# A down-projection computed as seven products of halved matrices instead of eight column-and-token blocks

## The chip, the core and the metric

The kernel runs on one core of a Trainium2 chip. A core has five engines with an instruction queue each, and each queue is worked off strictly in order: PE (TensorE, matrix products), DVE (VectorE), ACT (ScalarE), POOL (GpSimd), and SP (SyncE), which here only issues DMA transfers. Engines wait for each other through semaphores. SBUF is the on-chip memory of 128 partitions; PSUM is the accumulator memory of eight banks of 128x512 fp32 values, which PE writes. The metric is the device time of one execution in microseconds (us); less is better. TensorE's clock can be throttled; the profile gives the granted clock as a share of full speed.

## The reference

One layer of a diffusion backbone over 2048 latent tokens of width 1024 and 256 context tokens, batch 1, everything in fp32. A mixer (a 2-D Fourier branch and a bidirectional gated recurrence, merged by gates and projected) is followed by a convolutional feed-forward network of width 2816 on the 32x64 latent grid, and the result is normalised:

```python
def conv_ffn(h, w_up, conv_w, conv_b, w_down, rows, cols):
    z = (h @ w_up).reshape(b, rows, cols, 2 * D_FF)
    z = depthwise_3x3_conv(z, conv_w) + conv_b
    return (silu(z[..., :D_FF]) * z[..., D_FF:]) @ w_down

x = x + gate_2 * conv_ffn(modulate(rmsnorm(x, norm2_g), shift_2, scale_2), ...)
out = rmsnorm(x, final_g)
```

Here `gate_2` is a vector over the 1024 output columns (the sixth modulation vector, "m5" in the kernel), and `D_FF` is 2816 = 22 x 128. The change concerns the last product, 2048 x 2816 times 2816 x 1024, the gate behind it, the residual sum and the final norm.

## The kernel before, in words

fp32 matrices are multiplied with three matmuls of a faster format for each product: every operand is split into a high part (a cast by ACT) and a low part (raw minus high, by POOL or DVE), and PE adds high x high, high x low and low x high in PSUM (`split`, L100 to L103, `mm3`, L142 to L149). One matmul is a 128x128 stationary tile against 512 moving columns.

Earlier phases (projections, Fourier branch, recurrence, merge, output projection) are not touched. They leave the residual stream in 16 tiles `dX` in DRAM and the normalised input of the feed-forward network, split, in SBUF tiles of a pool with eight large slots H0 to H7.

**Up-projection** (`phase3`): for each of 22 pairs of 128-column blocks, two "halves" (gate column block and value column block), 44 in all. A half is 96 matmuls that fill four banks (`za` and `zb` alternate), over weights loaded by SP (two loads of 256 KB, `rw`), cast by ACT and subtracted by POOL (`load_w`). Two weight tiles exist, so the weights of half n+2 are split while half n+1 is computed. When a half's matmuls end, ACT computes the centre tap with the bias (`ac`, L1029) and one other tap (`be`, L1032) of the 3x3 convolution; DVE adds seven more taps from PSUM to `ac` (L1061), and only when they are done may the half after next write those four banks again; POOL adds `be` (L1037). Behind the second half ACT applies SiLU to the first, POOL multiplies the two (L1046, `gate`) and SP stores the result `dZ[j]`, 128x2048, to DRAM.

**Down-projection** (`down`): eight groups, two column halves by four groups of 512 tokens. A group runs over 22 blocks k of the feed-forward width with four banks, 12 matmuls a k: 2112 in all. `load_g` loads 128x512 of `dZ[k]`, ACT casts, POOL subtracts; `load_wd` does the same for the weights, and in the second column half multiplies them by `m5` beforehand. `evict` adds a finished bank to the residual that it loads from `dX`; the first column half goes back to DRAM (`dX2`) multiplied by the final norm's gain, and in the second column half each token tile is normalised and stored to the output.

The order in which instructions stand in each engine's queue is set by a scheduler from the program's order, from priorities and from when it expects operands and buffers to be ready; `issue_after` holds instructions back behind a named one. A buffer of a pool with `bufs=n` is reused in turn and waits for its last reader.

Of the kernel before, what the change touches and what calls it, by code (L numbers as in the profile page):

```python
# [94 lines left out]
class Layer:  # L95
# [56 lines left out]
    def run(self):  # L152
        tc, nc = self.tc, self.nc
        with ExitStack() as es:
# [14 lines left out]
            pr = tc.tile_pool(name="pr", bufs=1, reuse_waits="tile", side="right")  # L169
            self.pr = pr.__enter__()  # L170
# [3 lines left out]
            self.down(last, (p5, pw, pr))  # L174
            hpool.__exit__(None, None, None)

    def scratch(self):
# [15 lines left out]
        self.dX2 = [t([P, TB], f"dX2{i}") for i in range(16)]  # L193
# [806 lines left out]
    def phase3(self, p5):  # L1000


        tc, nc, a = self.tc, self.nc, self.a
        for j in range(NF):
            acc = []
            for half in range(2):
# [12 lines left out]
                end = jj == 2 * NF - 1  # L1019
                if end:  # L1020

                    self.wd, self.first = [], []
                    self.load_raw()
                    for k in range(6):
                        self.load_wd(0, k)
                        if k < 3:
                            self.first.append(self.load_g(0, k))
# [36 lines left out]
    def load_wd(self, gi, k, times=None):  # L1064

        c = gi // NB
        cs = slice(c * TB, (c + 1) * TB)
        src = self.a["ffn_down"]
        if k % 4 == 0:
            self.wt = self.ph.tile([P, 4, 2, TB], F32R, name=f"wd{c}{k}", tag=f"H{(6 * c + k // 4) % 8}")  # L1070
        w = self.wt[:, k % 4]
        if gi == 0:
            self.split(w[:, 0, :], w[:, 1, :], self.wraw[k], None if k < 8 else self.nc.vector)
        else:
            self.load_split(w[:, 0, :], w[:, 1, :], src[0, k * P:(k + 1) * P, cs], self.nc.vector, self.p6, 2, times, "wr")
        self.wd.append(w)

    def load_raw(self):


        self.wraw = []
        src = self.a["ffn_down"]
        for pool, tag, n in ((self.pw, "w", 4), (self.ph, "H6", 8), (self.ph, "H7", 8), (self.pw, "w", 2)):
            t = pool.tile([P, 8 if n == 8 else 4, TB], F32, name="wraw", tag=tag, bufs=1 if n == 8 else 2)
            for i in range(0, n, 2):
                k = len(self.wraw)
                self.nc.sync.dma_start(t[:, i:i + 2, :], src[0, k * P:(k + 2) * P, :TB].rearrange("(k p) c -> p k c", p=P))
                self.wraw += [t[:, i, :], t[:, i + 1, :]]

    def load_g(self, gi, k):  # L1090


        tg = gi % NB
        early = gi == 0 or gi == 1 and k < 3
        pool, nb = (self.pr, 3) if early else (self.p6, 5)
        gh = pool.tile([P, TB], F32R, name="gh", tag="gh", bufs=nb)
        gl = pool.tile([P, TB], F32R, name="gl", tag="gl", bufs=nb)
        if early and (gi or k >= 3):
            q = k if gi else (k - 3) % 4
            if q == 0:  # L1100
                self.graw = self.p5.tile([P, 4, TB], F32, name="graw", tag="be", bufs=2)
                for i in range(3 if gi else min(4, NF - k)):
                    self.last_load = self.nc.sync.dma_start(self.graw[:, i, :], self.dZ[k + i][:, tg * TB:(tg + 1) * TB])
            self.split(gh, gl, self.graw[:, q, :])
        else:
            self.load_split(gh, gl, self.dZ[k][:, tg * TB:(tg + 1) * TB], None, pool, 2 if early else 4)
        return gh, gl

    def down(self, last, pools):


        tc, nc, a = self.tc, self.nc, self.a
        wd = self.wd
        with ExitStack() as es:
            ps = []

            def evict(gi, accs):
# [111 lines left out]
```

## Time and profile before

| | us |
|---|---|
| median of three runs (lowest, highest) | 3133.27 (3123.41, 3134.48) |
| the profiled execution's own time | 3133.75 |
| its span, first to last instruction | 3131.9 |
| start of the up-projection's second half (first half's matmuls end) | 1688.4 |
| first matmul of the down-projection | 2623.8 |
| PE busy / DVE busy / POOL busy / ACT busy in the span | 3075.3 / 1750.7 / 963.4 / 935.8 |

The granted clock is 0.994 on average over the profiled execution. In the profile, a group of instructions is told by its line, engine, operation and tiles (out<-in), with count, busy time, mean length, and the idle time of that engine ahead of it with what ended it. PEld is the loading of stationary tiles, which runs beside the matmuls.

### The profile page before, as it was taken

What the parts mean: (1) busy time and instruction counts of PE and PEld (TensorE: products, weight loads), DVE (VectorE), ACT (ScalarE), POOL (GpSimd) and SP (SyncE); (2) the same over time, 40 slices, a digit from 0 to 9 for tenths busy, and PEclk for the clock granted to TensorE, in tenths of its full rate; (3) what the DMA queues carried; (4) which work ended last, traced back from release to release, by engine and by line L of the source; (5) the groups of instructions that cost most, each with busy time, mean ns of one, the idle gap of its engine ahead of it and who ended that gap; (6) DMA issues with size and microseconds to landing.
All of it is one profiled execution on the core that took longest, in us unless ns stands there. A gap on an engine that the chain in (4) does not pass through costs nothing.

```text
span 3131.9 us, 38972 instructions
## 1 busy us (share of the span) xinstructions
PE 3075.3 (98%) x14955; PEld 2561.1 (82%) x14955; DVE 1750.7 (56%) x2475; ACT 935.8 (30%) x1513; POOL 963.4 (31%) x568
## 2 busy tenths in 40 slices
PE   8999999999999999999999999999999999999998
PEld 5987788888888888877877888888888887788887
DVE  6365533566666640366665777777777777224113
ACT  4322111233333321234433222222222223223222
POOL 2200010000000001343443444344443446455443
PEclk9999999999999999999999999999999999999999
DMA  6255544423223322556561111111111114546443
GB/s 250 87 172 185 187 153 154 140 99 111 95 92 108 105 85 96 198 186 210 180 190 61 55 58 34 54 54 48 54 34 54 54 47 155 168 135 205 149 149 133
DMA packets 284043, 374.69 MB, mean 120 GB/s; under 512 B 20731, under 2 KB 158802, under 8 KB 279506
## 3 DMA queue, kind: packets, MB, share of 16 engines
q1 hardware_dynamic: 283666, 372.15, 36.0%
q8 instruction: 118, 1.93, 0.3%
q14 instruction: 67, 0.55, 0.1%
q0 software_dynamic: 192, 0.06, 0.0%
HBM read 270.68 MB, written 101.45 MB: 119 GB/s over the span
## 4 chain that ended last, share of the span: by engine, by line
PE 91%; DVE 4%; DMA 2%; issue 1%; ACT 1%; POOL 1%; SPq 0%; DVEq 0%; ACTq 0%; POOLq 0%
PE z L148 10%; PE z L147 10%; PE z L146 10%; PE pj L146 10%; PE pj L148 10%; PE pj L147 10%; PE dn L1198 5%; PE dn L1196 5%; PE dn L1197 5%; PE pa L788 4%; PE wo L946 2%; PE wo L947 2%; PE wo L945 2%; PE kv L660 1%; PE pj L379 1%
## 5 line engine op out<-in xcount | busy, mean ns | idle before, releaser
L1061 DVE SCALAR_TENSOR_TENSOR ac<-z,cw,ac 128x1953 f32<-128x1953 f32 (+2 forms) x309 | 703.0, 2275 | 257.0 <-ACT be L1032 242.4
L147 PE MATMUL z<-h,w_up 128*128 128x512 f32 x1408 | 548.8, 390 | 0.0
L146 PE MATMUL z<-h,w_up 128*128 128x512 f32 x1408 | 548.7, 390 | 0.0
L148 PE MATMUL z<-h,w_up 128*128 128x512 f32 x1408 | 548.7, 390 | 0.0
L1037 POOL TENSOR_TENSOR ac<-ac,be 128x1984 f32<-128x1984 f32 x43 | 192.4, 4474 | 434.5 <-DVE ac L1061 421.3
L147 PEld LDWEIGHTS z<-h,w_up 128*128 128x128 f32 x1408 | 264.4, 188 | 54.7
L148 PEld LDWEIGHTS z<-h,w_up 128*128 128x128 f32 x1408 | 264.4, 188 | 54.7
L146 PEld LDWEIGHTS z<-h,w_up 128*128 128x128 f32 x1408 | 264.4, 188 | 54.4
L1198 PE MATMUL dn<-wd,gl 128*128 128x512 f32 x704 | 279.2, 397 | 4.3 <-POOL gl L103 4.3
L1029 ACT ACTIVATE ac<-z,vt,cw 128x2048 f32<-128x2048 f32 x44 | 90.9, 2065 | 636.9 <-PE z L148 636.9
L1196 PE MATMUL dn<-wd,gh 128*128 128x512 f32 x704 | 279.0, 396 | 1.0 <-ACT gh L102 1.0
L103 POOL TENSOR_TENSOR gl<-rw,gh 128x512 fp32r<-128x512 f32 x154 | 207.2, 1353 | 233.6 <-ACT gh L102 213.6
L1197 PE MATMUL dn<-wd,gh 128*128 128x512 f32 x704 | 278.6, 396 | 0.0
L494 ACT ACTIVATE ev<-pj 128x512 f32<-128x512 f32 (+1 forms) x136 | 79.6, 585 | 369.0 <-PE pj L148 334.1
L102 ACT CAST gh<-rw 128x512 fp32r<-128x512 f32 x154 | 94.4, 618 | 245.6 <-PE dn L1197 179.1
L1198 PEld LDWEIGHTS dn<-wd,gl 128*128 128x128 f32 x704 | 133.3, 189 | 36.0 <-POOL gl L103 5.6
L1196 PEld LDWEIGHTS dn<-wd,gh 128*128 128x128 f32 x704 | 133.5, 190 | 31.9 <-ACT gh L102 1.4
L1197 PEld LDWEIGHTS dn<-wd,gh 128*128 128x128 f32 x704 | 133.6, 190 | 30.6
L103 POOL TENSOR_TENSOR w_up<-rw,w_up 128x512 fp32r<-128x512 f32 x88 | 112.8, 1306 | 90.6 <-ACT w_up L102 90.6
L788 PEld LDWEIGHTS pa<-bQ,bkc 128*128 128x128 f32 x896 | 120.6, 191 | 17.0 <-issue 10.6
L788 PE MATMUL pa<-bQ,bkc 128*128 128x128 f32 x896 | 127.5, 286 | 1.2
L103 POOL TENSOR_TENSOR wab<-rw,wab 128x512 fp32r<-128x512 f32 x64 | 93.5, 1480 | 110.4 <-ACT wab L102 110.4
(324 smaller groups left out, 6192.9 us busy)
## 6 DMA issues: line engine op xcount, KB each, us to landing
rw<-dZ SPq DMA_DIRECT2D x154, 256.0 KB, 3.2
rw<-in_ffn_up_dram SPq DMA_DIRECT2D x88, 256.0 KB, 3.6
dZ<-ac SPq DMA_DIRECT2D x22, 1024.0 KB, 4.4
rw<-in_w_in_dram SPq DMA_DIRECT2D x72, 256.0 KB, 3.2
maw<-in_ada_w_dram SPq DMA_DIRECT2D x64, 256.0 KB, 3.2
rw<-in_w_out_dram SPq DMA_DIRECT2D x64, 256.0 KB, 2.7
x<-dX SPq DMA_DIRECT2D x48, 256.0 KB, 5.4
x<-in_x_dram SPq DMA_DIRECT2D x20, 512.0 KB, 6.6
```

Of the source, the lines that this page charges most:

```text
L102: self.nc.scalar.copy(hi, raw)
L103: (eng or self.nc.gpsimd).tensor_tensor(lo, raw, hi, op=SUB)
L146: self.nc.tensor.matmul(ps, lh, rh, start=start and i == 0, stop=False)
L147: self.nc.tensor.matmul(ps, lh, rl, start=False, stop=False)
L148: mm = self.nc.tensor.matmul(ps, ll, rh, start=False, stop=stop and i == last)
L788: mm = nc.tensor.matmul(pa[:, c], kc[:, c], fap(Q, w * P, [(2 * m, nw), (W + m, 2), (1, m)]), start=True, stop=True)
L1029: self.centre = nc.scalar.activation(ac, z, AF.Identity, scale=self.cw[:, 4, jj:jj + 1], bias=self.v("cb", jj))
L1037: nc.gpsimd.tensor_tensor(ac[:, :SEQ - 64], ac[:, :SEQ - 64], be[:, 64:], op=ADD)
L1061: nc.vector.scalar_tensor_tensor(o, z3[:, r0 + dy:r1 + dy, c0 + dx:c1 + dx], self.cw[:, k, jj:jj + 1], o, op0=MUL, op1=ADD)
L1196: nc.tensor.matmul(accs[i], gh[:, t], wh, start=(kk == 0), stop=False)
L1197: nc.tensor.matmul(accs[i], gh[:, t], wl, start=False, stop=False)
L1198: nc.tensor.matmul(accs[i], gl[:, t], wh, start=False, stop=(kk == NF - 1))
```

## The change

The product of the gated activations G (2048 x 2816) and the weights W (2816 x 1024) is cut into halves of the tokens, of the feed-forward width and of the columns. Instead of eight products of quarter matrices, seven are formed, each from sums or differences of at most two quarters of G and of at most two quarters of W, and each is added to or subtracted from up to two quarters of the result (`PRODUCTS`). One product covers 1024 tokens in all eight banks, 11 steps k of 24 matmuls: 7 x 11 x 24 = 1848 matmuls.

- A step's operands (`operand`): one or two loads of 512 KB of `dZ`, a DVE sum or difference of 128x1024 where there are two, a cast and a POOL subtraction of 128x1024; one or two loads of 256 KB of weights, a DVE sum or difference of 128x512 where there are two, a cast and a POOL subtraction of 128x512. They are asked for five steps ahead. Of the seven products, the third and sixth have two quarters of G and one of W, the fifth one and two, the second, fourth and seventh two and two. The first has one quarter of G, and its weights are prepared beforehand.
- The gate m5 is multiplied into all of `ffn_down` beforehand (`gated_weights`, 22 pieces: SP loads 512 KB, POOL multiplies 128x1024 by m5, SP stores 512 KB to `dV5`), and the first product's weights are prepared beforehand too (`first_weights`, 11 pieces: two loads of 256 KB, a POOL subtraction, a split, and a store to `dW` issued by POOL). Both stand inside the up-projection: the program names them at its halves 5 to 26 and 29 to 39. The pieces share two buffers `ws`, and the split one buffer `wsr`.
- The residual lies in four quarter tiles in SBUF, in slots of the H pool; a finished bank is added to them (`evict`, one or two DVE instructions of 128x512 a bank). The reload through `dX2` and the DVE multiplication by m5 in the down-projection are gone. The second half of the tokens is normalised during the sixth product (`half_done`), the rest bank by bank at the end.
- In the last two steps of a product (five in the last product) the matmuls go bank by bank.

```diff
                 end = jj == 2 * NF - 1
+                jt = 2 * j + half
+                if 4 <= jt < 4 + NF:
+                    self.gated_weights(p5, jt - 4)
+                elif 28 <= jt < 28 + KH:
+                    self.first_weights(p5, jt - 28)
                 if end:
-                    self.load_raw()
...
+                    self.first_operands(p5, range(3))
                 self.centre = nc.scalar.activation(ac, z, AF.Identity, ...)
...
-    def load_wd(self, gi, k, times=None):
-    def load_raw(self):
-    def load_g(self, gi, k):
...
+    def gated_weights(self, p5, k):
+        raw = p5.tile([P, D], F32, name="ws", tag="ws", bufs=2)
+        nc.sync.dma_start(raw, self.a["ffn_down"][0, k * P:(k + 1) * P, :])
+        nc.gpsimd.tensor_tensor(raw, raw, self.m5, op=MUL)
+        nc.sync.dma_start(self.dV5[k], raw)
+
+    def first_weights(self, p5, k):
+        raw = p5.tile([P, 2, TB], F32, name="ws", tag="ws", bufs=2)
+        self.load_terms(raw, self.weight_terms(PRODUCTS[0], k))
+        nc.gpsimd.tensor_tensor(raw[:, 1, :], raw[:, 1, :], raw[:, 0, :], op=SUB)
+        w = p5.tile([P, 2, TB], F32R, name="wsr", tag="wsr", bufs=1)
+        self.split(w[:, 0, :], w[:, 1, :], raw[:, 1, :])
+        nc.gpsimd.dma_start(self.dW[k], w)
+
+    def operand(self, idx):
+        p, k = divmod(idx, KH)
+        prod = PRODUCTS[p]
...
+        w = self.p6.tile([P, 2, TB], F32R, name="w", tag="w", bufs=6)
+        rg = self.p6.tile([P, 2, 2 * TB], F32, name="rg", tag="rg", bufs=3)
+        self.load_terms(rg, [self.dZ[KH * kh + k][:, 2 * th * TB:2 * (th + 1) * TB] for th, kh, _ in prod[0]])
+        if p == 0:
+            nc.gpsimd.dma_start(w, self.dW[k])
+        else:
+            rw = self.p6.tile([P, 2, TB], F32, name="rv", tag="rv", bufs=3)
+            self.load_terms(rw, self.weight_terms(prod, k))
+        if len(prod[0]) == 2:
+            nc.vector.tensor_tensor(rg[:, 1, :], rg[:, 1, :], rg[:, 0, :], op=prod[0][1][2])
+        self.split(g[:, 0, :], g[:, 1, :], rg[:, 1, :])
+        if p:
+            if len(prod[1]) == 2:
+                nc.vector.tensor_tensor(rw[:, 1, :], rw[:, 1, :], rw[:, 0, :], op=prod[1][1][2])
+            self.split(w[:, 0, :], w[:, 1, :], rw[:, 1, :])
+
+    def product(self, idx, acc, i):
+        nc.tensor.matmul(acc, gh[:, t], wh, start=(k == 0), stop=False)
+        nc.tensor.matmul(acc, gh[:, t], wl, start=False, stop=False)
+        nc.tensor.matmul(acc, gl[:, t], wh, start=False, stop=(k == KH - 1))
...
+            def evict(p, i):
+                for th, c, op in PRODUCTS[p][2]:
+                    x = X[th, c][:, i, :]
+                    nc.vector.tensor_tensor(x, x, accs[i], op=op)
+                if p < 6:
+                    return
+                square(0, 0, i)
...
+            for p in range(7):
...
+                late = 2 if p < 6 else 5
+                for k in range(8 if p == 0 else 0, KH):
+                    idx = KH * p + k
+                    if idx + AHEAD < 7 * KH:
+                        self.operand(idx + AHEAD)
+                    if k < KH - late:
+                        for i in range(8):
+                            self.product(idx, accs[i], i)
...
+                for i in range(8):
+                    for k in range(KH - late, KH):
+                        self.product(KH * p + k, accs[i], i)
+                    evict(p, i)
+
+PRODUCTS = [([(0, 0, ADD)], [(0, 1, ADD), (1, 1, SUB)], [(0, 1, ADD), (1, 1, ADD)]),
...
+KH, AHEAD = NF // 2, 5
```

The scheduler does not leave the new pieces at the halves at which the program names them. All 22 gated pieces and all 11 of the first product's weights stand within the first eleven halves of the up-projection, in the queues of SP, POOL and ACT. First, POOL's queue. Before, from the addition of `be` of the third half on (`gl` is the low part of a first operand of the down-projection):

```order
L1037 TENSOR_TENSOR ac<-ac,be 128x1984
L103 TENSOR_TENSOR w_up_14818<-rw,w_up_14818 128x512 x2
L1037 TENSOR_TENSOR ac<-ac,be 128x1984
L1046 TENSOR_TENSOR ac<-ac 128x2048
L103 TENSOR_TENSOR w_up_14939<-rw,w_up_14939 128x512 x2
L103 TENSOR_TENSOR gl<-rw,gh 128x512
```

The same stretch with the change. The line numbers have shifted by two (L1039 is the addition of `be`, L1048 the gate product); L1071 is the product with m5, L1079 the subtraction in `first_weights`, L1082 its store:

```order
L1039 TENSOR_TENSOR ac<-ac,be 128x1984
L1071 TENSOR_TENSOR ws<-ws,m_14232 128x1024
L103 TENSOR_TENSOR w_up_14838<-rw,w_up_14838 128x512 x2
L1071 TENSOR_TENSOR ws<-ws,m_14232 128x1024 x4
L1039 TENSOR_TENSOR ac<-ac,be 128x1984
L1048 TENSOR_TENSOR ac<-ac 128x2048
L1071 TENSOR_TENSOR ws<-ws,m_14232 128x1024 x2
L103 TENSOR_TENSOR w_up_14963<-rw,w_up_14963 128x512 x2
L1079 TENSOR_TENSOR ws<-ws 128x512
L103 TENSOR_TENSOR wsr<-ws,wsr 128x512
```

So the low parts of the weights for the next halves (w_up_14838 for the sixth half, w_up_14963 for the seventh) now stand behind products with m5, each of which needs a landed load and a buffer that a store has freed.

Second, ACT's queue with the change, from the split of the seventh half's weights on (before, it holds only the casts `w_up`, `ac`, `be` and the SiLU there):

```order
L102 CAST w_up_14963<-rw 128x512 x2
L102 CAST wsr<-ws 128x512 x2
L1031 ACTIVATE ac<-z,vt,cw 128x2048
L1034 ACTIVATE be<-z,cw 128x2048
L1036 ACTIVATE ac<-ac 128x2048
L102 CAST w_up_15085<-rw 128x512 x2
L102 CAST wsr<-ws 128x512 x4
L1031 ACTIVATE ac<-z,vt,cw 128x2048
L1034 ACTIVATE be<-z,cw 128x2048
```

The casts into `wsr`, which has one buffer that only the store to `dW` frees, stand ahead of the centre tap (L1031) of the sixth half, and four more ahead of that of the seventh.

Third, DVE's queue at the end of the first product (L1132 and L1136 are the sums of the next product's operands, L1212 the additions of finished banks to the quarter tiles):

```order
L1136 TENSOR_TENSOR rv<-rv 128x512
L1132 TENSOR_TENSOR rg<-rg 128x1024 x2
L1136 TENSOR_TENSOR rv<-rv 128x512
L1132 TENSOR_TENSOR rg<-rg 128x1024
L1212 TENSOR_TENSOR x_19865<-x_19865,dn 128x512
L1136 TENSOR_TENSOR rv<-rv 128x512
L1212 TENSOR_TENSOR x_19874<-x_19874,dn 128x512
```

Additions to the result now stand between operand sums that wait for loads; before, no DVE instruction of the down-projection's operands had two loaded terms.

More of the change, by code (lines that the diff above doesn't have):

```diff
@@ L173, in run @@
             last = self.phase3(self.p5)
-            self.down(last, (p5, pw, pr))
+            self.down(last, (p5, pw))
             hpool.__exit__(None, None, None)
@@ L192, in scratch @@
         self.dS0 = [t([P, P], f"dS0{h}") for h in range(4)]
-        self.dX2 = [t([P, TB], f"dX2{i}") for i in range(16)]
+        self.dW = [dr.tile([P, 2, TB], F32R, name=f"dW{k}") for k in range(KH)]
+        self.dV5 = [t([P, D], f"dV5{k}") for k in range(NF)]
         self.dU = t([P, 16, TB], "dU")
@@ L1003, in phase3 @@
         tc, nc, a = self.tc, self.nc, self.a
+        self.m5 = p5.tile([P, D], F32, name="m5")
+        nc.sync.dma_start(self.m5, self.dm5)
         for j in range(NF):
@@ L1078, in load_raw @@
-    def load_raw(self):
[L1081 to L1088, printed above, removed]
@@ L1090, in load_g @@
-    def load_g(self, gi, k):
[L1093 to L1107, printed above, removed]
+    def gated_weights(self, p5, k):
+        nc = self.nc
+        raw = p5.tile([P, D], F32, name="ws", tag="ws", bufs=2)
+        nc.sync.dma_start(raw, self.a["ffn_down"][0, k * P:(k + 1) * P, :])
+        nc.gpsimd.tensor_tensor(raw, raw, self.m5, op=MUL)
+        nc.sync.dma_start(self.dV5[k], raw)
@@ new lines, in down @@
+            z4 = [pool.tile([P, SEQ], F32, name="dn", tag="z") for pool in (self.za, self.zb)]
+            accs = [z4[i // 4][:, (i % 4) * TB:(i % 4 + 1) * TB] for i in range(8)]
+            p5 = self.p5
+            with tc.issue_after(self.centre.ins):
+                self.first_operands(p5, range(3, 4))
+                self.first_operands(p5, range(4, 8))
+            for k in range(8):
+                for i in range(4):
+                    self.product(k, accs[i], i)
+            last()
@@ new lines, in down, with load_quarter @@
+            for q in pools:
+                q.__exit__(None, None, None)
+            p6 = self.p6 = es.enter_context(tc.tile_pool(name="p6", bufs=1, reuse_waits="tile"))
+            fg = p6.tile([P, D], F32, name="fg")
+            ss = p6.tile([P, 2, 16], F32, name="ss")
+            X = {}
+            def load_quarter(th, c, tag):
+                X[th, c] = self.ph.tile([P, 8, TB], F32, name=f"x{th}{c}", tag=tag)
+                for i in range(8):
+                    nc.sync.dma_start(X[th, c][:, i, :], self.dX[8 * th + i][:, c * TB:(c + 1) * TB])
```

198 lines of the change are left out of this document (99 added, 99 removed).

## The prediction

> **What bounds the kernel now.** The slices of the page come first, then the chain that ended last, then windows in the two stages that the change touches.
>
> ```profile
> PE   8999999999999999999999999999999999999998
> PE 91%; DVE 4%; DMA 2%; issue 1%; ACT 1%; POOL 1%; SPq 0%; DVEq 0%; ACTq 0%; POOLq 0%
> ```
>
> PE is busy in every slice and carries 91% of the chain. So matmuls that go away are worth their full pitch, and a wait put in front of PE costs its full length. Next, two windows of 100 us (span and sum, then PE, PEld, DVE, ACT, POOL busy with counts, granted clock, DMA share, GB/s), the first in the up-projection, the second in the down-projection, and the down-projection's matmuls by tile:
>
> ```profile
> 2300.00:2400.00 100.00, 100.00 (x443) 82.85 (x442) 74.96 (x33) 25.93 (x21) 45.17 (x18) 1.00 0.18 58
> 2800.00:2900.00 100.00, 100.00 (x432) 81.19 (x431) 38.53 (x58) 34.63 (x66) 50.11 (x36) 1.00 0.55 180
> L1196 PE MATMUL dn<-wd,gh x704: 388/393/629, 2623.8 to 3121.8; 128*128 128x512 f32 x176
> ```
>
> PE has no gap in either. A matmul overlaps the next, so its price is the pitch: 100/443 = 0.2257 us, with the last one's overlap about 0.2266, in the up-projection (a half of 96 is 21.75 us), and 100/432, with the same correction 0.2324 us, in the down-projection. That stage lasts from 2623.8 to the span's end at 3131.9: 508.1 us.
>
> **The change part by part.** Removed: 2112 - 1848 = 264 matmuls, 264 x 0.2324 = 61.4 us. The remaining ones take 1848 x 0.2324 = 429.5 us; bounds are 0.2266 (418.8) and, if the pitch grows with DMA traffic as it does between the two windows (0.0058 us for 0.37 of DMA share; a step of up to 1.5 MB in 5.58 us is about 280 GB/s, a share near 0.85), 0.2371 (438.2).
>
> Operands of a step must be ready every 24 x 0.2324 = 5.58 us. Prices on POOL come from the up-projection:
>
> ```profile
> L103 POOL TENSOR_TENSOR w_up<-rw,w_up 128x512 fp32r<-128x512 f32 x82 | 104.7, 1301 | 75.7 <-ACT w_up L102 75.7
> L1046 POOL TENSOR_TENSOR ac<-ac 128x2048 f32<-128x2048 f32 x20 | 92.6, 4630 | 1.6
> ```
>
> 1.30 us for 512 columns and 4.63 for 2048 make 2.17 ns a column, so 1024 columns take 2.41 us, and POOL needs 2.41 + 1.25 to 1.30 = 3.7 us a step. DVE's two sums are estimated from rows of the down-projection's timeline (start, length of the group, engine, line, operation, tiles, count, wait ahead), where POOL and DVE collide, and one row by tile:
>
> ```profile
> 2649.80 9.29 POOL L103 TENSOR_TENSOR gl<-graw,gh 128x512 fp32r<-128x512 f32 x2 [1.10 <-ACT gh L102]
> 2649.63 1.88 DVE L103 TENSOR_TENSOR wd<-wraw,wd 128x512 fp32r<-128x512 f32 x3
> 2651.43 2.28 DVE L1046 TENSOR_TENSOR ac<-ac 128x2048 f32<-128x2048 f32 x1
> 2653.64 3.08 DVE L103 TENSOR_TENSOR wd<-wraw,wd 128x512 fp32r<-128x512 f32 x5
> L1136 DVE TENSOR_TENSOR x<-dn,x x16: 682/692/693, 2936.6 to 3123.4; 128x512 f32<-128x512 f32 x16
> ```
>
> A sum of 512 is 3.08/5 = 0.6 us, one of 1024 half of 2.28, 1.13 us: 1.74 a step. Two POOL subtractions that take 2.6 us alone took 9.29 while DVE ran 7.24 us of instructions with both inputs in SBUF: they exclude each other. The additions out of PSUM (L1136) kept 0.69 us each, all 16, so they do not. With exclusion a step costs 3.65 + 1.74 = 5.39 us in the products with two quarters on both sides, 4.8 in those with one sum of 1024, 4.25 in the fifth: under 5.58, narrowly. The Trainium skill, "SBUF — State Buffer", section "Who interferes with whom", says the same against this change: a DVE instruction with two SBUF inputs locks out a GpSimd instruction that reads SBUF, whole instruction by whole instruction, and one with a single SBUF input does not. By it the sum would be the 5.39 above, the trace agrees with its 9.29, and its reach to evictions is a rival below.
>
> A product's evictions are up to 16 x 0.69 = 11.0 us of DVE in the 11.2 us of its last two steps, staggered bank by bank, so the next product's first bank is free in time. I add 12 us for waits in the stage: some 5 between the first and second products, whose sums wait for loads ahead of evictions in DVE's queue, 3.5 at the last product's steps that are consumed bank by bank, and 3.5 for the clock that such waits cost. Bounds are 5 (only one such wait) and 38. What the clock costs is seen in the timeline behind a long wait of the stage before, with a window of 3 us there; the last three rows are the timeline's end:
>
> ```profile
> 2657.89 0.50 PE L1198 MATMUL dn<-wd,gl 128*128 128x512 f32 x1 [2.75 <-POOL gl L103]
> 2660.00:2663.00 3.00, 3.00 (x8) 2.32 (x8) 0.00 (x0) 0.62 (x1) 1.61 (x2) 0.53 0.00 0
> 3123.44 0.69 DVE L1136 TENSOR_TENSOR x<-dn,x 128x512 f32<-128x512 f32 x1
> 3127.11 0.75 DVE L1144 SCALAR_TENSOR_TENSOR x<-x,rs_y,fg 128x512 f32<-128x512 f32 x1
> 3128.28 0.38 SPq L1145 DMA_DIRECT2D out_dram<-x  x1
> ```
>
> A wait of 2.75 us is followed by matmuls at a granted 0.53 (8 in 3 us), about 1.7 us lost. The tail is 3131.9 - 3122.4 = 9.5 us from the last matmul to the end. Afterwards eight banks pass through it one after the other, 3.9 us of DVE a bank against 15 matmuls = 3.49 of PE, so 11.5. The stage becomes 429.5 + 12 + 11.5 = 453.0, 55.1 us less than 508.1. The DVE multiplications by m5 and the reload of the residual that go were hidden under PE: nothing for them.
>
> **Added to the up-projection** are 22 and 11 pieces on SP, POOL and ACT, whose averages leave room (POOL 45 of 100 us). Where they stand in the queues decides. The stage's own rhythm, half 5 (counted from one) and its neighbours:
>
> ```profile
> 1774.04 4.47 POOL L1037 TENSOR_TENSOR ac<-ac,be 128x1984 f32<-128x1984 f32 x1 [11.44 <-DVE ac L1061]
> 1783.18 2.54 POOL L103 TENSOR_TENSOR w_up<-rw,w_up 128x512 fp32r<-128x512 f32 x2
> 1688.38 2.06 ACT L1029 ACTIVATE ac<-z,vt,cw 128x2048 f32<-128x2048 f32 x1 [3.13 <-PE z L148]
> 1775.37 2.06 ACT L1029 ACTIVATE ac<-z,vt,cw 128x2048 f32<-128x2048 f32 x1 [14.88 <-PE z L148]
> 1797.27 2.07 ACT L1029 ACTIVATE ac<-z,vt,cw 128x2048 f32<-128x2048 f32 x1 [5.79 <-PE z L148]
> 1779.33 16.14 DVE L1061 SCALAR_TENSOR_TENSOR ac<-z,cw,ac 128x2016 f32<-128x2016 f32 x7 [5.43 <-ACT be L1032]
> ```
>
> Halves end at 1688.4, 1775.4, 1797.3, every 21.8 us. The seventh half's weights are split at 1783.2 and wanted at 1797.3: 14 us of slack. The taps take 16.1 us behind `ac` and `be` (4), ending at 1795.5, 1.8 us before the half after next wants their banks: nearly no slack, so whatever holds `ac` back holds PE back. The added transfers are priced by rows of the DMA issues (the last figure is us from issue to landing):
>
> ```profile
> rw<-in_ffn_up_dram SPq DMA_DIRECT2D x88, 256.0 KB, 3.6
> wraw<-in_ffn_down_dram SPq DMA_DIRECT2D x11, 512.0 KB, 4.8
> rw<-in_w_out_dram SPq DMA_DIRECT2D x64, 256.0 KB, 2.7
> out_dram<-x SPq DMA_DIRECT2D x32, 256.0 KB, 2.3
> dX<-x SPq DMA_DIRECT2D x16, 512.0 KB, 4.2
> dZ<-ac SPq DMA_DIRECT2D x22, 1024.0 KB, 4.4
> vr<-in_ada_b_dram POOLq DMA_DIRECT2D x1, 24.0 KB, 5.2
> vr<-in_norm_g_dram POOLq DMA_DIRECT2D x2, 4.0 KB, 3.6
> ```
>
> I take 3.6 us for a load, 3.0 for a store of 512 KB (between 2.3 and 4.4), 4 for POOL's own store. Two `ws` buffers then turn once in 3.6 + 2.4 + 3.0 and issue, 9.4 us a pair. Following the queues row by row with these: (a) from 1776 POOL does four products with m5, paced by their loads, until 1791.7, then the late `be` addition (1796.2), the gate (1800.9), two more products (1805.7), and the seventh half's first weights at 1807.0: PE waits 10 us from 1797.1. (b) The casts into the single `wsr` stand ahead of the sixth half's `ac`: subtraction, cast, split and store of one piece must pass before the second cast, `ac` starts at 1824.3 and its taps end at 1844.5 for 1828.9: 16 us. (c) The next two halves' `ac` stand behind four casts each, every one a round of about 6 us: 7 and 8 us. Together 41 us; slow clock behind the first three waits only uses up part of the next, behind the last it adds 1.7: **42.5 us**. With every leg at its shortest row (2.7, 2.0, 2.0) it is 24, since (b) and (c) remain; at the longest (4.8, 4.2, 5.8) 74. In a sentence apart: the Trainium skill, "DMA: Bandwidth & Descriptors", section "Anatomy of one DMA — SWDGE (gpsimd) path", fits such a POOL-queue transfer as 2.0 us plus bytes/436e3 (in us), 3.2 us for 512 KB; no run here shows one of this size, and the estimate by it would be 39 instead of 42.5.
>
> Sum: -55.1 + 42.5 = -12.6. The profiled execution took 3133.75, 0.5 over the median, so 3133.3 - 12.6 = 3120.7, say **3120**.
>
> **The rivals.**
> *The queues absorb the preparation.* If loads land early because SP runs far ahead, and the casts find their data, only (b)'s first rounds and one of (c) remain, at most 20 us: 3133 - 55 + 17 = 3095. For it: POOL idles more than half of the stage (the 45.17 above) and DMA's share is 0.18. Against it: the rows stand in order, and one `wsr` buffer forces a round trip through DRAM stores whatever the averages.
> *POOL and DVE become the bound of the down-projection* (the other side). If the additions out of PSUM exclude POOL after all, products of two and two quarters cost 11 x 5.39 + 11.0 = 70.3 us of the pair against 61.4 of PE, 9 each in three, 2.4 each in two, and some 5 to 9 at boundaries: 28 us; with 0.1 us lost at each of a step's four handovers, 50. Then 3133 - 55 + 42.5 + 28 to 50 = 3149 to 3170, 3158 in the middle. It decides as soon as evictions count: without them the step stays under 5.58. Against it stands the unstretched L1136, for it that the skill's page speaks of one shared pair.
> *Fewer matmuls, no faster.* With all eight banks cycling and a step's traffic of 280 GB/s the pitch would have to rise to 0.2324 + 61.4/1848 = 0.266 us to eat the gain: about 3134 with the stall partly overlapped. The pitch has never been above 0.2324 for long at full clock.
>
> **How the numbers follow.** Forecast 0.55 (its own range 3098 to 3152, from the stall's 24 to 74 with the sum else as taken), absorbed queues 0.25, POOL and DVE as bound 0.14, no faster 0.06. A measurement here tells about 0.5%, 15.7 us: faster is below 3117.6, slower above 3148.9. Faster: 0.20 of the forecast's (its lower half with short transfers) + 0.24 = 0.44. Slower: 0.05 + 0.13 + 0.01 = 0.19. Same: 0.37. The range reaches down to the absorbed case with the lower pitch (3095 less 7: 3088) and up to the middle of the other side, 3155.
>
> **What would show it.** The up-projection's 44 halves: PE idle before the seventh to tenth, released by w_up's split once and by DVE's taps three times, total 24 to 74; fewer than 20 means absorption. POOL groups of `dW` stores and `wsr` casts waiting for each other. In the down-projection 1848 matmuls in about 441 us, POOL's subtractions of 1024 at 2.4 us when alone; if they reach 4 in the products with two sums while evictions run, the third rival holds. Wrong would be waits elsewhere, above all at product boundaries or in the last product, beyond the 12 and 11.5 us.

## The result: 3155.26 us, slower by 0.8%

| | before | changed |
|---|---|---|
| median of five runs, us | 3133.27 (3123.41 to 3134.70) | 3155.26 (3149.89 to 3159.31) |
| ratio | | 1.0077, 95% interval 1.0057 to 1.0098 |
| profiled execution: span, mean granted clock | 3131.9, 0.994 | 3151.7, 0.985 |

The page of the changed kernel, its slices of PE and the chain that ended last:

```profile
PE   8999999999999999999999868999999999999998
PE 31%; POOL 4%; DMA 4%; DVE 3%; issue 2%; ACT 1%; SPq 0%; POOLq 0%; DVEq 0%; ACTq 0%
```

Before, every slice read 9 but the first and last; now three slices stand at 8, 6 and 8. PE carries 31% of the chain instead of 91%, POOL and DMA 4% each instead of 1% and 2%. (A chain's shares cover the part that could be followed back, so they need not add up to the whole.) Two windows tell the place of the loss, from the up-projection's first matmul to the down-projection's, and from there to the span's end. First before, then changed (the stretch and its length, then PE, PEld, DVE, ACT and POOL busy with counts, granted clock, DMA share, GB/s):

```profile
1659.90:2623.80 963.90, 961.76 (x4257) 796.21 (x4256) 701.54 (x332) 266.71 (x217) 412.36 (x163) 1.00 0.17 53
2623.80:3131.90 508.10, 493.61 (x2113) 399.92 (x2111) 154.03 (x339) 161.96 (x295) 247.97 (x178) 0.99 0.48 159
```

```profile
1656.20:2687.30 1031.10, 974.11 (x4257) 802.74 (x4256) 701.49 (x332) 272.66 (x224) 499.79 (x221) 0.97 0.26 84
2687.30:3151.70 464.40, 440.02 (x1849) 351.62 (x1847) 305.90 (x356) 144.16 (x214) 305.88 (x145) 0.97 0.73 253
```

The up-projection, whose matmuls are the same, takes 67.2 us more: PE is idle for 57.0 instead of 2.1, and the same matmuls are busy for 12.4 us more, at a granted clock of 0.97. The down-projection takes 43.7 us less. The phases ahead of both came out 3.7 us shorter; their start moves by several us from program to program (1651.7 to 1662.6 in the kernels of this study), so experiments below are compared by stage. 67.2 - 43.7 - 3.7 = 19.8, the difference of the spans.

PE's timeline has five long waits in the up-projection of the changed kernel (start, length, what, then the wait ahead and what ended it):

```profile
1776.77 0.80 PE L146 MATMUL z<-h,w_up 128*128 128x512 f32 x1 [4.92 <-ACT w_up L102]
1811.81 0.80 PE L148 MATMUL z<-h,w_up 128*128 128x512 f32 x1 [10.13 <-POOL w_up L103]
1852.77 0.77 PE L146 MATMUL z<-h,w_up 128*128 128x512 f32 x1 [17.64 <-DVE ac L1063]
1887.94 0.77 PE L146 MATMUL z<-h,w_up 128*128 128x512 f32 x1 [11.40 <-DVE ac L1063]
1923.39 0.76 PE L146 MATMUL z<-h,w_up 128*128 128x512 f32 x1 [10.60 <-DVE ac L1063]
```

Together they are 54.7 us, ahead of the sixth to tenth half (the second comes two matmuls into the seventh). The first goes through two queues. On POOL a product with m5 waits for its load, and the `be` addition stands behind it; on ACT the SiLU waits 20.31 us for that addition, and the casts of the sixth half's weights stand behind the SiLU:

```profile
1767.51 2.40 POOL L1071 TENSOR_TENSOR ws<-ws,m 128x1024 f32<-128x1024 f32 x1 [4.70 <-DMA ws<-in_ffn_down_dram]
1774.30 1.91 ACT L1036 ACTIVATE ac<-ac 128x2048 f32<-128x2048 f32 x1 [20.31 <-POOL ac L1039]
1776.12 1.12 ACT L102 CAST w_up<-rw 128x512 fp32r<-128x512 f32 x2
```

What stands behind the second wait is on POOL's timeline, the seventh half's weights (L103, 1810.49) behind products with m5 that wait for loads, the `be` addition, the gate product and two more products with m5:

```profile
1792.15 4.78 POOL L1071 TENSOR_TENSOR ws<-ws,m 128x1024 f32<-128x1024 f32 x2 [6.18 <-DMA ws<-in_ffn_down_dram]
1796.88 4.49 POOL L1039 TENSOR_TENSOR ac<-ac,be 128x1984 f32<-128x1984 f32 x1
1801.45 4.50 POOL L1048 TENSOR_TENSOR ac<-ac 128x2048 f32<-128x2048 f32 x1
1805.90 4.64 POOL L1071 TENSOR_TENSOR ws<-ws,m 128x1024 f32<-128x1024 f32 x2
1810.49 2.50 POOL L103 TENSOR_TENSOR w_up<-rw,w_up 128x512 fp32r<-128x512 f32 x2
```

Behind the fourth, on ACT's timeline, stands the seventh half's centre tap (L1031, 1867.70; its matmuls ended long before). It comes behind casts into the one `wsr`, each waiting for the store to `dW` of the piece before:

```profile
1851.58 0.62 ACT L102 CAST wsr<-ws 128x512 fp32r<-128x512 f32 x1 [8.85 <-DMA dW<-wsr]
1859.55 0.62 ACT L102 CAST wsr<-ws 128x512 fp32r<-128x512 f32 x1 [7.36 <-DMA dW<-wsr]
1867.18 0.62 ACT L102 CAST wsr<-ws 128x512 fp32r<-128x512 f32 x1 [7.01 <-DMA dW<-wsr]
1867.70 2.06 ACT L1031 ACTIVATE ac<-z,vt,cw 128x2048 f32<-128x2048 f32 x1
```

A round takes 8 us. POOL's rows divide the one that begins at 1851.58: the store is issued 2.7 us later (1854.25, since the split stands behind the next piece's subtraction), and 5.3 us after that the next cast starts. The transfers of both kinds of pieces, from the DMA issues (KB each, median us from issue to landing):

```profile
ws<-in_ffn_down_dram SPq DMA_DIRECT2D x22, 512.0 KB, 4.1
dV<-ws SPq DMA_DIRECT2D x22, 512.0 KB, 2.9
dW<-wsr POOLq DMA_DIRECT2D x11, 512.0 KB, 5.1
```

In the down-projection PE waits at the end of the first product, ahead of the last product and in its last steps, 14.2 us in all over the rows of PE's timeline (5.3 before). One of the longest of each place:

```profile
2742.88 0.50 PE L1145 MATMUL dn<-w,g 128*128 128x512 f32 x1 [3.49 <-DVE x L1212]
3069.34 0.76 PE L1145 MATMUL d<-w,g 128*128 128x512 f32 x1 [3.56 <-DVE x L1212]
3114.24 0.80 PE L1146 MATMUL d<-w,g 128*128 128x512 f32 x1 [2.57 <-POOL w L103]
```

DVE's timeline ahead of the last product: sums (L1132, L1136) that wait for loads, and behind them the evictions that PE waits for.

```profile
3053.32 1.72 DVE L1132 TENSOR_TENSOR rg<-rg 128x1024 f32<-128x1024 f32 x1 [3.99 <-DMA rg<-dZ]
3062.77 1.22 DVE L1132 TENSOR_TENSOR rg<-rg 128x1024 f32<-128x1024 f32 x1 [6.03 <-DMA rg<-dZ]
3067.13 1.46 DVE L1132 TENSOR_TENSOR rg<-rg 128x1024 f32<-128x1024 f32 x1 [1.78 <-DMA rg<-dZ]
3070.20 8.45 DVE L1212 TENSOR_TENSOR x<-x,d 128x512 f32<-128x512 f32 x14
```

### The profile page after: what moved, and what is told of

Same layout as the page of the kernel before. It is cut to its first block, busy times and chain, and to the rows that moved or that the text cites. A ratio compares the mean times of both kernels' runs of the same rounds, so it can differ in the third digit from the quotient of the medians.

```text
span 3151.7 us, 38316 instructions
## 1 busy us (share of the span) xinstructions
PE 3029.1 (96%) x14691; PEld 2514.3 (80%) x14691; DVE 1901.9 (60%) x2492; ACT 924.1 (29%) x1439; POOL 1110.4 (35%) x593
## 5 line engine op out<-in xcount | busy, mean ns | idle before, releaser
L146 PE MATMUL z<-h,w_up 128*128 128x512 f32 x1408 | 553.0, 393 | 44.6 <-DVE ac L1063 39.6
L148 PE MATMUL z<-h,w_up 128*128 128x512 f32 x1408 | 552.0, 392 | 10.3 <-POOL w_up L103 10.1
L1039 POOL TENSOR_TENSOR ac<-ac,be 128x1984 f32<-128x1984 f32 x43 | 192.1, 4467 | 363.4 <-DVE ac L1063 363.4
L1031 ACT ACTIVATE ac<-z,vt,cw 128x2048 f32<-128x2048 f32 x44 | 90.9, 2065 | 609.8 <-PE z L148 609.8
L1145 PE MATMUL d<-w,g 128*128 128x512 f32 x528 | 211.1, 400 | 5.0 <-DVE x L1212 4.8
L1146 PE MATMUL d<-w,g 128*128 128x512 f32 x528 | 210.5, 399 | 3.4 <-POOL w L103 3.4
L1147 PE MATMUL d<-w,g 128*128 128x512 f32 x528 | 210.1, 398 | 0.0
L103 POOL TENSOR_TENSOR g<-rg,g 128x1024 fp32r<-128x1024 f32 x69 | 183.1, 2665 | 61.9 <-ACT g L102 61.8
L1132 DVE TENSOR_TENSOR rg<-rg 128x1024 f32<-128x1024 f32 x55 | 97.1, 1768 | 79.7 <-DMA rg<-dZ 75.9
L103 POOL TENSOR_TENSOR w_up<-rw,w_up 128x512 fp32r<-128x512 f32 x88 | 112.5, 1300 | 76.1 <-ACT w_up L102 76.1
L103 POOL TENSOR_TENSOR wab<-rw,wab 128x512 fp32r<-128x512 f32 x64 | 93.8, 1485 | 111.4 <-ACT wab L102 111.4
L103 POOL TENSOR_TENSOR w<-rv,w 128x512 fp32r<-128x512 f32 x66 | 108.5, 1648 | 57.8 <-ACT w L102 54.8
L1145 PEld LDWEIGHTS d<-w,g 128*128 128x128 f32 x528 | 100.4, 190 | 32.0 <-DVE x L1212 4.6
L793 DVE COPY_PREDICATED bA<-mask,pa 128x512 f32<-128x512 uint8 x112 | 82.6, 738 | 71.2 <-PE pa L787 70.2
```

The lines of the kernel that those rows point to most:

```text
L103: (eng or self.nc.gpsimd).tensor_tensor(lo, raw, hi, op=SUB)
L146: self.nc.tensor.matmul(ps, lh, rh, start=start and i == 0, stop=False)
L148: mm = self.nc.tensor.matmul(ps, ll, rh, start=False, stop=stop and i == last)
L1031: self.centre = nc.scalar.activation(ac, z, AF.Identity, scale=self.cw[:, 4, jj:jj + 1], bias=self.v("cb", jj))
L1039: nc.gpsimd.tensor_tensor(ac[:, :SEQ - 64], ac[:, :SEQ - 64], be[:, 64:], op=ADD)
L1132: nc.vector.tensor_tensor(rg[:, 1, :], rg[:, 1, :], rg[:, 0, :], op=prod[0][1][2])
```

## Experiments on the up-projection

The theory is that the loss is a matter of order. Pieces of work that wait for transfers stand in in-order queues ahead of work that PE needs next. Two rivals are that the added work or traffic costs it wherever it stands, and that one of the two kinds of pieces makes all of it.

**Both kinds held at their halves.** The helper calls are put behind named instructions, nothing else:

```diff
+                    self.adds.append(nc.gpsimd.tensor_tensor(ac[:, :SEQ - 64], ...))
...
+                    with tc.issue_after(self.adds[-2].ins):
                         self.gated_weights(p5, jt - 4)
...
+                    with tc.issue_after(self.adds[-2].ins), tc.issue_after(self.below.ins):
                         self.first_weights(p5, jt - 28)
```

(`self.below` is the ACT instruction that makes `be`.)

> The change, with the added pieces held in the queues at about the halves at which the program names them: one gated piece, or one piece of the first product's weights, in each half of the up-projection (their POOL instructions behind the addition of `be` of the half before last, their ACT casts behind `be` of the half before). The same instructions, buffers and bytes are left. Theory (order in the queues): PE's waits of 54.7 us in the up-projection fall to under 5 us, the slow clock behind them goes too, the stage takes 963 to 968 us as before, and the down-projection stays at 464: 3155 - 65 = 3090 us, between 3084 and 3100. Rival (the added work or traffic itself, wherever it stands): waits of 40 us or more stay, 3140 to 3155.

3088.67 us (3083.57 to 3090.20), ratio to the kernel before 0.9856 (0.9839 to 0.9873). The two windows:

```profile
1658.10:2622.00 963.90, 961.74 (x4257) 795.76 (x4256) 701.54 (x332) 272.06 (x224) 499.58 (x221) 1.00 0.27 90
2622.00:3086.90 464.90, 438.04 (x1849) 351.48 (x1847) 305.32 (x356) 144.15 (x214) 306.20 (x145) 0.98 0.73 253
```

The up-projection takes 963.90 us, as before the change, with POOL's 499.58 us of work and a DMA share of 0.27 where the change had 499.79 and 0.26. In the trace the gated pieces now come one every 22 us (POOL, 1754.7 to 2211.9) and the first product's weights likewise (2276.9 to 2494.5). So the work and the traffic are free there, and their place and density in the queues cost all 67.2 us. The down-projection is as in the change. This version is faster than both kernels.

**One kind held.** The same edit, once for the first product's weights alone, once for the gated pieces alone.

> As the run above, but only the first product's weights are held at their halves; the 22 gated pieces stand early and dense as in the change. Theory: the waits before the sixth and the seventh half, which the gated pieces make (4.9 and 10.1 us, and 4 of slow clock), stay, the three released by DVE's taps (39.6 us and 7 of clock) go: about 3155 - 47 = 3108. Rival: the gated pieces are the cause of all five waits because everything behind them is late: 3145 or more.

> Only the 22 gated pieces are held, one a half; the pieces of the first product's weights then follow in bunches of two or three in ACT's queue ahead of a half's centre tap, some 25 halves later than in the change. Theory: the casts that wait for the one buffer hold the centre taps there, a round being 8 us: three or four waits of 4 to 12 us, 25 to 35 together, 3115 to 3125. Rival (the gated pieces are the whole cause): no waits, 3090.

The times are 3107.14 and 3122.16 us, one execution each. PE's long waits, first with the gated pieces left early, then with the first product's weights left dense:

```profile
1778.98 0.79 PE L146 MATMUL z<-h,w_up 128*128 128x512 f32 x1 [4.83 <-ACT w_up L102]
1813.07 0.79 PE L148 MATMUL z<-h,w_up 128*128 128x512 f32 x1 [9.29 <-POOL w_up L103]
```

```profile
2235.31 0.77 PE L146 MATMUL z<-h,w_up 128*128 128x512 f32 x1 [6.43 <-DVE ac L1065]
2268.90 0.77 PE L146 MATMUL z<-h,w_up 128*128 128x512 f32 x1 [10.02 <-DVE ac L1065]
2303.61 0.77 PE L146 MATMUL z<-h,w_up 128*128 128x512 f32 x1 [10.87 <-DVE ac L1065]
```

Each kind makes waits of its own: the gated pieces the first two, the casts into `wsr` three more, which come some 380 us later in the second run and are 27.3 us instead of 39.6. The stage takes 983.4 and 996.9 us, 19.5 and 33.0 over the 963.9. These make 52.5 of the 67.2 us; the other 14.7 arise only where both kinds stand dense together. One meeting is seen in the changed kernel, where POOL's first subtraction of the first product's weights waits 9.23 us for a load of `dV` behind the last gated pieces; how the 14.7 divide is open.

**The round's longest leg.** ACT's order is kept, only the store's queue is another:

```diff
-        nc.gpsimd.dma_start(self.dW[k], w)
+        nc.sync.dma_start(self.dW[k].bitcast(F32), w.bitcast(F32))
```

> The change with one edit: the store of a piece to `dW` is issued by SP instead of POOL; ACT's order is the same. In the trace POOL's store takes 5.1 us from issue to landing and SP's stores of 512 KB 2.9. Theory (the length of a round sets the third to fifth wait): a round shrinks from 8 to about 6 us; following the queues by hand with the measured legs gives waits of 15, 6 and 8 us instead of 17, 10 and 12, that is 9 us less: about 3146. If the round is set by the loads of the next piece instead, nothing changes: 3155.

The time is 3143.32 us, one execution. The store by the DMA issues, and two rounds on ACT's timeline:

```profile
dW<-wsr SPq DMA_DIRECT2D x11, 512.0 KB, 3.0
```

```profile
1857.27 0.62 ACT L102 CAST wsr<-ws 128x512 fp32r<-128x512 f32 x1 [4.45 <-DMA dW<-wsr]
1862.31 0.62 ACT L102 CAST wsr<-ws 128x512 fp32r<-128x512 f32 x1 [4.42 <-DMA dW<-wsr]
```

A round is 5 us, the stage 1017.2 us instead of 1031.1, and PE's third to fifth wait are 13.1, 3.5 and 6.4 us instead of 17.6, 11.4 and 10.6: 16.7 us less, more than the 9 expected. The length of a round sets these waits, and the store was the largest part of it: its 2.1 us make most of the 3 that a round lost. The stage itself gained 13.9 us, less than the waits, because PE was busy for 3.1 us more (977.2 against 974.1).

## Experiments on the down-projection

All stand on the version with both kinds held, most with one execution (the kernel before had medians of 3129.0 to 3133.1 us beside them); its stage takes 464.9 us, of which 16.8 are waits of PE (summed over its timeline) and 8.5 slow clock behind them (438.04 us busy against 429.52 in the run without waits below). Five kernels of this study differ in the up-projection alone, and their down-projections took 463.8 to 467.0 us in the trace. A row within 3 us of 464.9 therefore shows no effect.

| edit | stage, us | all, us |
|---|---|---|
| none (both kinds held) | 464.9 | 3088.67 (4 runs) |
| second half's output stores issued by ACT | 467.5 | 3084.83 |
| first product's accumulators as eight tiles | 463.4 | 3084.09 |
| these two together | 465.3 | 3086.02 (4 runs) |
| late operands behind the evictions | 476.9 | 3102.44 |
| late operands behind, and eight tiles | 464.8 | 3089.90 (4 runs) |
| four buffers for raw activations | 459.9 | 3085.81 (4 runs) |
| no sums (other output) | 440.0 | 3065.95 |
| sums with one load (other output) | 467.9 | 3094.25 |

**Without the sums.**

```diff
-        if len(prod[0]) == 2:
-            nc.vector.tensor_tensor(rg[:, 1, :], rg[:, 1, :], rg[:, 0, :], op=prod[0][1][2])
...
-            if len(prod[1]) == 2:
-                nc.vector.tensor_tensor(rw[:, 1, :], rw[:, 1, :], rw[:, 0, :], op=prod[1][1][2])
```

> paced_both without DVE's sums of operands: where a product needs the sum of two quarters, both are loaded, but only the first is used, so the output is not the layer's. It measures what DVE and POOL cost each other. Theory (they exclude each other, but stay within PE's budget): POOL's subtractions fall from 2.67 to 2.41 us (1024) and from 1.65 to 1.30 (512), the pitch of the matmuls between the second and the sixth product stays at 0.233, and only the waits at the ends of the first and sixth product shrink, because evictions no longer stand behind sums: 3075 to 3082. Rival (the pair of engines is the bound of the stage): the pitch falls and the stage loses 28 us or more, 3060 or less.

The stage's window comes first. Then come POOL's subtractions from 2720 to 3060 us in groups (count, busy time, mean ns, idle time ahead), without sums and, in the third fence, with them and with DVE's sums of 1024:

```profile
2623.70:3063.70 440.00, 429.52 (x1849) 347.21 (x1847) 146.11 (x257) 143.87 (x214) 268.51 (x145) 0.99 0.75 267
```

```profile
L103 POOL TENSOR_TENSOR g<-rg,g 128x1024 fp32r<-128x1024 f32 x54 | 131.4, 2449 | 16.4 <-ACT g L102 16.4
L103 POOL TENSOR_TENSOR w<-rv,w 128x512 fp32r<-128x512 f32 x55 | 72.6, 1324 | 85.6 <-ACT w L102 61.3 <-DMA rv<-dV 15.5 <-DMA rg<-dZ 8.8
```

```profile
L103 POOL TENSOR_TENSOR g<-rg,g 128x1024 fp32r<-128x1024 f32 x56 | 147.6, 2647 | 37.7 <-ACT g L102 37.6
L103 POOL TENSOR_TENSOR w<-rv,w 128x512 fp32r<-128x512 f32 x57 | 92.6, 1629 | 56.6 <-ACT w L102 56.6
L1135 DVE TENSOR_TENSOR rg<-rg 128x1024 f32<-128x1024 f32 x44 | 78.2, 1780 | 72.1 <-DMA rg<-dZ 70.8 <-POOL w L103 1.3
```

Every wait of the stage is gone, also those in the last steps, and the pitch is the same (429.52/1848 = 0.2324 us). The stage is 24.9 us shorter, more than expected. DVE and POOL do stretch each other: POOL's mean is 2.65 against 2.45 us and 1.63 against 1.32, and a sum of 1024 takes 1.78, where the prediction had 1.13. Rows by tile give the lowest, median and highest ns of the stage with sums. The longest sum exceeds the shortest by 2.27 us, about one POOL subtraction, and the longest subtraction exceeds the shortest by 1.05 us, less than one sum:

```profile
L103 POOL TENSOR_TENSOR g<-rg,g x69: 2343/2409/3393, 2656.0 to 3046.6; 128x1024 fp32r<-128x1024 f32 x69
L1135 DVE TENSOR_TENSOR rg<-rg x55: 1206/1693/3474, 2664.0 to 3041.5; 128x1024 f32<-128x1024 f32 x55
```

Yet between the products' ends PE does not wait for it. The rival that expected a shorter pitch is out, and it is shown that the waits need the sums. The amount of traffic alone does not make them, since it was no less here (267 GB/s against 253).

**How the sums make PE wait** was asked in seven runs. The first three remove obstacles at single places:

> paced_both with one more edit: the output stores of the second half of the tokens, which are made during the sixth product, are issued by ACT instead of SP. Theory: ahead of the last product PE waits (5.7 and 0.6 us, and slow clock behind) because SP's queue holds operand loads behind eight stores that wait for the normalisation, so DVE's sums wait for loads and the evictions stand behind the sums. Without the stores in SP's queue these waits go, and with them some of the 3.4 us in the last steps: 8 to 12 us less than 3088.7, about 3079. Rival (the transfers themselves are too many there, DMA share 0.7 to 0.8): nothing changes.

> paced_both with one more edit: the first product's eight accumulators are eight tiles of one bank, as in the other products, instead of two tiles of four banks. Theory: at the end of the first product a bank's matmuls wait for the eviction of the bank before in the same tile (3.5, 2.0 and 1.5 us of waits and about 4 of slow clock), since the wait is kept by tile; with a tile a bank they go: 7 to 10 us less than 3088.7, about 3080. Rival, as the prediction had it (operand sums that wait for loads hold up the evictions): the waits move to the first steps of the second product and the time stays at 3089.

> Both edits of the two runs above on paced_both. Theory: the gains add, the down-projection takes about 447 us instead of 464: 3070, between 3066 and 3076. If one of the waits is only shifted: 3079.

```diff
-                nc.sync.dma_start(self.out[ti * P:(ti + 1) * P, ...], X[th, c][:, i, :])
+                (nc.scalar if th else nc.sync).dma_start(self.out[ti * P:(ti + 1) * P, ...], X[th, c][:, i, :])
```

```diff
-            z4 = [pool.tile([P, SEQ], F32, name="dn", tag="z") for pool in (self.za, self.zb)]
+            accs = [bank(i) for i in range(4)]
...
+            accs += [bank(i) for i in range(4, 8)]
```

The theory on the stores fell. With them on ACT the wait ahead of the last product grew from 5.7 to 11.3 us. ACT's casts now stand behind stores that wait for the normalisation, here one cast between three stores and five:

```profile
2970.92 0.62 ACT L102 CAST w<-rv 128x512 fp32r<-128x512 f32 x1 [9.12 <-DVE x L1202]
3004.74 0.77 PE L1148 MATMUL d<-w,g 128*128 128x512 f32 x1 [11.27 <-DVE x L1215]
```

With eight tiles the waits around the first product's end are 3.0 us instead of 6.9, so part of them was a wait kept by tiles of four banks. The stage is 1.5 us shorter where 7 to 10 were expected, which is within the spread. (`bank` gives a tile of one bank, [P, TB].) The two edits together gain nothing.

The next two runs change the order in DVE's queue:

```diff
-                    if idx + AHEAD < 7 * KH:
+                    if idx + AHEAD < 7 * KH and k < KH - 2:
                         self.operand(idx + AHEAD)
...
                     evict(p, i)
+                    if p < 6 and i in (3, 7):
+                        with tc.issue_after(self.added_to.ins):
+                            self.operand(KH * p + KH - 2 + i // 4 + AHEAD)
```

> paced_both with one more edit: the operands of a product's fourth and fifth step are asked for behind the evictions of the product before (DVE's sums behind the fourth and the eighth bank's), not ahead of them. Theory: without any sums the down-projection, from its first matmul to the span's end, took 440.0 us instead of 464.9, because sums that wait for loads stand ahead of evictions in DVE's queue; with evictions ahead of at least these two steps' sums the 6.3 us of waits before the last product and a part of the 6.9 at the first one's end go, with their slow clock: the stage takes 452 to 458 us. Rival (the sums are late for POOL's sake and whatever the order, so that waits only move to the next product's fourth step): 463 or more.

> evictions_first with the first product's accumulators as eight tiles of one bank. Theory: the waits at the first product's end, which are kept by tiles of four banks (6.9 us before, 3.0 with a tile a bank), go too: the stage takes 448 to 454 us, 3072 to 3080 in all. Rival: as above, 3084 or more.

The stage takes 476.9 and 464.8 us: the waits move to other products' ends and into the last steps. The theory that the place of two steps' sums decides fell too. The last two runs change the loads and the buffers (`load_one` loads a sum's first quarter alone, for activations and weights):

```diff
-        self.load_terms(rg, [...])
+        self.load_one(rg, [...])
```

> paced_both, where a product needs the sum of two quarters the second quarter is not loaded, and DVE adds the first to itself: as many sums of the same size and place in DVE's queue, with both inputs in SBUF, but each waits for one load and a third of the stage's traffic is gone. The output is not the layer's. It tells apart what makes the waits of the down-projection, which were all gone without the sums. If sums that wait for loads are it (late loads ahead of evictions in DVE's queue): waits under 2 us, the stage takes 440 to 444 us. If DVE and POOL locking each other out is it, whatever the loads: waits of 10 us or more stay, 455 to 465.

```diff
-        rg = self.p6.tile([P, 2, 2 * TB], F32, name="rg", tag="rg", bufs=3)
+        rg = self.p6.tile([P, 2, 2 * TB], F32, name="rg", tag="rg", bufs=4)
```

> paced_both with four instead of three buffers for the raw activations (rg), so that loads can be issued a step earlier. If late loads are what DVE's sums and the evictions behind them wait for: the waits shrink by half or more, the stage takes 450 to 456 us instead of 465, 3074 to 3080 in all. If the loads are late because DMA or SP is late in itself, or if the lock of DVE and POOL decides: 463 or more, 3087 or more.

```profile
2624.60:3092.50 467.90, 436.57 (x1849) 350.57 (x1847) 325.39 (x356) 142.51 (x214) 312.64 (x145) 0.97 0.51 165
```

```profile
2619.30:3079.20 459.90, 436.20 (x1849) 350.55 (x1847) 306.88 (x356) 144.05 (x214) 307.49 (x145) 0.98 0.74 256
```

With a DMA share of 0.51 instead of 0.73, the waits stay (31.3 us of the stage without a busy PE, against 26.9), although DVE's sums of 1024 now wait 48 us for loads instead of 79. The stage is longer than either theory expected. So it is not the amount of traffic. With a fourth buffer the stage is 5.0 us shorter, between the two forecasts, in one trace, which is the fastest of four executions; their median is 0.9856 of the kernel before, as with three buffers, so a gain is not shown. What is shown is that without the sums the stage is 25 us shorter. The two runs point to the sums' 159 us of DVE (305 against 146 us busy) beside POOL rather than to their loads: a chain of load, sum, cast, subtraction and a freed buffer would have little slack where 16 evictions come on top. That chain is argued and not shown. How much of it is the two engines' exclusion and how much the sums' mere length on DVE stays open; no run has sums that POOL does not feel.

## Why the prediction was wrong, step by step

The forecast was 12.6 us less, and the median came out 22.0 us more (3155.26 against 3133.27). The prediction had the places and the kind of the waits mostly right, and it sized three terms too small: the waits of the up-projection, the slow clock behind them, and the waits of the down-projection.

- **What bounds the kernel, and 61.4 us for 264 matmuls: right.** The pitch stayed (0.2324 without sums), and a DMA share of 0.73 instead of 0.48 did not raise it; the bound of 0.2371 did not come up.
- **Where the up-projection stalls: right in place and kind but for one.** The prediction had waits of 10, 16, 7 and 8 us before the seventh to tenth half, one ended by POOL's split and three by DVE's taps; measured 10.1, 17.6, 11.4 and 10.6, ended so. The 4.9 us before the sixth half, ended by its cast, were put at nothing: the step looked at what stands ahead of the weights on POOL, not at ACT's SiLU, which waits for POOL's late `be` addition and holds the casts behind it.
- **The rounds were taken too short.** The prediction had about 6 us for a round with 4 for POOL's store; measured 8, with 5.1 for the store and the split held behind the next piece's subtraction. With the wait before the seventh half as forecast, nearly all of the 8.8 us missing on these four waits is in the three that the rounds make. The gated pieces' load and store, 4.1 and 2.9 us against 3.6 and 3.0, still let a pair turn in 9.7 us (POOL's products at 1698.40 and 1708.07) against 9.4. Followed again with the measured figures, the queues give 3, 12, 17, 10 and 12 us, an estimate of 54 made after the result, where 54.7 were measured. POOL's store was put at 4 between rows of a few KB at 3.6 and 5.2. The Trainium skill's "DMA: Bandwidth & Descriptors", section "Anatomy of one DMA — SWDGE (gpsimd) path", gives an estimate of 3.2 us for it, farther off still; the measurement decides.
- **The slow clock was taken at 1.7 us and cost 12.4.** The step "slow clock behind the first three waits only uses up part of the next" failed. Each of the five waits was followed by a loss of its own, 2.5 us on average, and none was earned back: the next half's end, its centre tap and the next deadline move along with the late matmuls.
- **The waits of the down-projection: 12 forecast, 25 measured** (14.2 of waits, 10.5 of clock); the tail, 11.5, took about 10. The place at the first product's end was named, and there the four-bank tiles had a part that was not seen; the wait ahead of the last product was not forecast. The bounds of 5 and 38 held it. That the sums are needed for these waits is shown; by which step of the chain they delay PE stays open.
- **The rivals.** "The queues absorb the preparation" is what happens once the pieces are spread (3088.67 against its 3095), not with this order: the argument against it, that the rows stand in order, was the right one. "POOL and DVE become the bound" is refuted in its own form: additions out of PSUM keep their 0.67 to 0.69 us, and PE is not slowed between the products' ends. The exclusion of sums and subtractions that the Trainium skill's "SBUF — State Buffer", section "Who interferes with whom", states is seen in the 2.65 against 2.45 us and in sums of 1.2 to 3.5 us. "Fewer matmuls, no faster" is refuted by the stage's 43.7 us.
- **The range.** The stall's 24 to 74 us held the measured 67.2, and 5 to 38 held the 25. But the forecast's own range let the stall vary with the rest as taken, and both terms came out high. Its upper end of 3155 came from the rival on POOL and DVE; that the time fell beside it is chance and speaks for nothing in that rival.
- **Slips in the working.** With a stall of 24 us the sum is 3102, not 3098. The rival's 28 us do not follow from its terms, which make 37 to 41 (three of 9, two of 2.4, and 5 to 9), unless the 12 of waits already counted are taken off. Its middle is given as 3158 and used as 3155. None of these changes the account above.

So the sum -55.1 + 42.5 should have read -43.7 + 67.2. Of the 36 us between, 5 are the wait before the sixth half, 9 the longer rounds, 11 the clock of the up-projection and 11 the down-projection's waits; the 3.7 us of earlier start go the other way.

## What to carry to other kernels

Work that is free by an engine's average can cost its whole waiting time when it stands in an in-order queue ahead of what the bounding engine needs next: look at who stands behind each added instruction that waits for a transfer, and spread such pieces one to a period behind a named instruction. Follow that through every queue on the way: here a late addition on POOL held a SiLU on ACT, and the SiLU held the casts. When a chain of round trips is priced, take rows of the same size and queue where there are any, and the longer one between two; and give each long wait of the bounding engine its own loss of clock. Sums of operands, the price of saving one product in eight, are not hidden by being short: without them the stage was 25 us shorter here, against the 61 that the missing matmuls bring, although no engine but PE was full.

## What the runs showed of the hardware

The same store of 512 KB to `dW` took 4.6 to 5.1 us (medians) from issue to landing when POOL issued it and 3.0 when SP did; other stores of 512 KB by SP took 2.6 to 4.2.

Behind each of the five waits of 5 to 18 us in the changed kernel, matmuls came every 0.43 us instead of 0.23 for 3.8 to 6.1 us. By their starts each stretch lost 1.8 to 2.9 us, 1.8 behind the longest wait; PE's busy time of the stage grew by 12.4, 2.5 a wait. The granted clock of 3 us right behind the longest wait:

```profile
1852.77:1855.77 3.00, 3.00 (x7) 2.42 (x8) 0.00 (x0) 0.00 (x0) 1.76 (x2) 0.50 0.20 66
```

A shorter wait was not always followed by this: after 3.47 us at the first product's end (both kinds held) the next twelve matmuls came every 0.23 us.

POOL's subtractions of 1024 columns took 2.45 us on average without operand sums and 2.65 beside sums of two SBUF inputs. Those sums took 1.21 us at the least, 1.78 on average and 3.47 at the most. Additions of 512 columns out of PSUM kept 0.67 to 0.69 us.
